# One attention layer and one retention layer in split fp32: residual loads, first-group loads, a v split, moves on ScalarE and squares in two parts

## The chip, the cores and the metric

The kernel runs on one core of one Trainium2 chip. A core has five engines that run their own instruction streams and meet at semaphores: TensorE (PE; its weight loads are listed apart as PEld), VectorE (DVE), ScalarE (ACT), GpSimd (POOL) and SyncE (SP). Of SP only the DMAs that it issues matter here; POOL issues DMAs too. The metric is device microseconds (us) of one execution, the median of 3 runs; lower is better.

## The reference

Batch 1, 512 tokens, width 2048, two layers. What is computed:

```python
# layer 0: gated grouped-query attention, 16 heads of 128, 4 k/v heads
proj = h @ w_in                                   # 2048 -> q 2048, k 512, v 512, g 2048
q = apply_rope(rms_norm(q, q_gain), cos, sin) * (A_HEAD_DIM ** -0.5)
k = apply_rope(rms_norm(k, k_gain), cos, sin)
s = q k^T ; p = softmax(s) ; o = p v              # in blocks of 128 queries
y = (o * jax.nn.silu(g)) @ w_out
x = layer_norm(ALPHA * x + y, ln_gain[0], ln_bias[0])
# layer 1: gated bidirectional retention, 8 heads, q/k 256, v 512
proj = h @ w_in                                   # 2048 -> q 2048, k 2048, v 4096, g 4096
o = forward scan(q, k, v) + backward scan(q, k, v)
y = (head_group_norm(o) * jax.nn.silu(g)) @ w_out
x = layer_norm(ALPHA * x + y, ln_gain[1], ln_bias[1])
```

All is fp32, and the layer norms keep mean and variance of a row of 2048 elements: `mean((x - mu)**2)` with `mu = mean(x)`.

## The kernel before

**Products.** Every fp32 operand is split into a high part `hi` (rounded to fp32r by a ScalarE cast, L114) and a low part `lo = x - hi` (a VectorE subtraction, L115), and a product is three matmuls, hi·hi, lo·hi and hi·lo (`mm3`, L232 to L234). Weights come in chunks of 128x1024 fp32 (512 KB): `raw_load` (L122) asks for a chunk on SP's queue, `onto` (L126) adds another quarter to it with a DMA that POOL issues, `make_chunk` splits it into `whi` and `wlo`, and 12 matmuls of 512 columns use it. `next_chunk` makes chunks up to AHEAD = 2 ahead of the one in use; `wp` holds three split chunks, `rp` nine raw ones. The large input products are done blockwise by a seven-product scheme: each block of 1024 output columns is worked off as products 1 to 7 in the order (1, 5, 6, 3, 7, 2, 4), each of 4 chunks, 7 x 4 x 12 matmuls in all; L160 and L162 add weight quarters on VectorE, L277 to L283 add input quarters, and `spill` adds the results up.

**Order of work.** The order on TensorE is the order in which the program is written. For the other engines a scheduler sets it when the kernel is built, from the same program and its own estimates; each engine then works strictly in that order, so an instruction that waits holds up all that stand behind it on its engine.

**Stages.** (1) Layer 0's input product, blocks `a_in`; q, k, v and g are stored to DRAM. (2) Attention: `Group.load_kv` and `load_q` read them back and split them (k, v and q tiles), while `work`, a stream of leftover products, is pumped between the attention's steps so that TensorE has work; `work.pump(us)` takes so many microseconds of it, counted as MM3 = 0.68 per triple of matmuls. The last block of `a_in` is the stream under group 0. (3) Layer norm 1 (`norm_1`): its result is stored to `nD`, turned by TensorE transposes, and moved from PSUM to SBUF with gain and bias in `turn_1`, 128x256 at a time: 16 moves for each half r of the tokens, of which the odd k go to VectorE (L823) and the even to ScalarE (L826). `x2.form` then adds quarters (L277 to L283). (4) Layer 1's input product, 12 blocks `r_in`: for each pair of heads two q/k/v blocks and one gate block. `residual_2` hangs on four of these blocks through `hook`: for a slice c of 512 columns and a token tile t it loads gain and bias of layer norm 1 (for t = 0, L836) and the stored `nD` (L839), multiplies and adds on VectorE (L837, L840, L841) and stores ALPHA times the normed x to `yD2` (L842, issued by POOL), onto which the output products add later. It hangs on blocks 2 to 5, before the third chunk of product 1, 6, 3 or 2. (5) The heads (`Head.run`): `s_unit` makes a strip of scores and splits it (pTh, pTl), `o_unit` multiplies with v; `v.split` splits the two v tiles (inh, inl). Heads 0 and 1 run with the last `r_in` block as their stream, the others with output products. (6) The last output product in four token tiles, each with layer norm 2 right behind it (`norm_2`): sums of the rows come with the additions (`add`, L386), the squares from ScalarE (L421), `1/sqrt` from a POOL power (L450); z = (y - mu) gain on VectorE (L1023), y = z rstd + bias (L1026), then the store.

**Lines that the change touches.** L846 `hook(r_in[2 + c], (1, 6, 3, 2)[t], 2, residual_2, c, t)`; L749 `work.pump(31.5 * MM3)` ahead of `groups[0].load_kv()`; L822 `if k % 2:` in `turn_1`; L983 `if kb > 1 and len(self.v.tiles) < 2:` in `Head.run`; L411 to L424 `mean_rstd`.

Of the kernel before, what the change touches and what calls it, by code (L numbers as in the profile page):

```python
# [50 lines left out]
def encoder_trunk_kernel(  # L51
# [313 lines left out]
    class Sum:  # L365


        def __init__(self, quick=()):

            self.y, self.st, self.rows, self.quick = {}, {}, [], quick  # L370

        def load(self, src, halves=(0, 1)):
            for i in halves:
# [7 lines left out]
        def add(self, t, c, ps, scale, last=False):  # L381
# [9 lines left out]
                nc.vector.tensor_add(y, ps, y)  # L391
            if last and t in self.quick:
                nc.vector.bn_stats(self.st[t][:, 6 * c:6 * c + 6], y)

        def out_proj(self, og, scale, cols=(0, 1, 2, 3), last=False):

            for c in cols:
# [11 lines left out]
                for t in range(NT):  # L409
                    self.add(t, c, banks[t], scale, last)  # L410

        def mean_rstd(self, t):

            if t in self.quick:
                return mean_rstd(self.st[t])
            mu, neg, sq, rstd = small("k_rs", 4)[:, 0:1], small("nmr"), small("sm", 4), small("rstd")
            nc.vector.tensor_reduce(out=mu, in_=self.st[t][:, :4], axis=AX.X, op=ALU.add)
            nc.vector.tensor_scalar_mul(neg, mu, -1.0 / D)
            nc.vector.tensor_scalar_mul(mu, mu, 1.0 / D)
            for c in range(4):  # L420
# [390 lines left out]
    def turn_1(r, m):  # L811
# [7 lines left out]
        for k in (2 * m, 2 * m + 1):  # L819
            o = 256 * (k % 2)  # L820
            f = x2.quarter(r, kh, i)[:, k % 4]
            if k % 2:  # L822
                nc.vector.tensor_scalar(f, b[:, o:o + 256], lnt[:, 0, k:k + 1], lnt[:, 1, k:k + 1],  # L823
                                        op0=ALU.mult, op1=ALU.add)
            else:
                nc.scalar.activation(f, b[:, o:o + 256], AF.Identity, scale=lnt[:, 0, k:k + 1], bias=lnt[:, 1, k:k + 1])  # L826
        if r == 0 and m % 2:
            x2.form(1 + kh, i)

    def residual_2(c, t, gb={}):  # L830

        cs = slice(c * 512, c * 512 + 512)
        if t == 0:
            for n in ("ln_gain", "ln_bias"):
                gb[n] = temp(n)
                nc.sync.dma_start(out=gb[n], in_=a[n][0, cs].partition_broadcast(P))  # L836
            nc.vector.tensor_scalar_mul(gb["ln_bias"], gb["ln_bias"], ALPHA)  # L837
        f = temp("res")
        nc.sync.dma_start(out=f, in_=nD[:, t, cs])  # L839
        nc.vector.scalar_tensor_tensor(out=f, in0=f, scalar=ALPHA, in1=gb["ln_gain"], op0=ALU.mult, op1=ALU.mult)  # L840
        nc.vector.tensor_add(f, f, gb["ln_bias"])  # L841
        nc.gpsimd.dma_start(out=yD2[:, t, cs], in_=f)  # L842
# [68 lines left out]
    class Head:  # L911
# [240 lines left out]
```

## Time and profile before

| | us |
|---|---|
| median of 3 runs | 2148.22 (2147.92 to 2150.19) |
| the profiled execution, its own time | 2150.57 |
| its span, first to last instruction | 2148.8 |
| PE busy in the span | 2108.5 (98%) |
| DVE busy | 1604.8 (75%) |
| ACT busy | 1100.8 (51%) |
| POOL busy | 377.2 (18%) |

TensorE is busy almost throughout, so the time is its work plus the places where it stands still or runs at a lower clock. A timeline row gives an instruction's start, its duration, and in brackets how long the engine sat idle before it and what ended that. Matmuls overlap, so their pace is read from start to start, not from durations. The profiled execution took 2.35 us more than the median.

### The profile page before, as it was taken

What the parts mean: (1) busy time and instruction counts of PE and PEld (TensorE: products, weight loads), DVE (VectorE), ACT (ScalarE), POOL (GpSimd) and SP (SyncE); (2) the same over time, 40 slices, a digit from 0 to 9 for tenths busy, and PEclk for the clock granted to TensorE, in tenths of its full rate; (3) what the DMA queues carried; (4) which work ended last, traced back from release to release, by engine and by line L of the source; (5) the groups of instructions that cost most, each with busy time, mean ns of one, the idle gap of its engine ahead of it and who ended that gap; (6) DMA issues with size and microseconds to landing.
All of it is one profiled execution on the core that took longest, in us unless ns stands there. A gap on an engine that the chain in (4) does not pass through costs nothing.

```text
span 2148.8 us, 26395 instructions
## 1 busy us (share of the span) xinstructions
PE 2108.5 (98%) x9744; PEld 1739.3 (81%) x9744; DVE 1604.8 (75%) x2185; ACT 1100.8 (51%) x1453; POOL 377.2 (18%) x449
## 2 busy tenths in 40 slices
PE   8999999999999999999999999999999999999997
PEld 7778887888888877788888888888888778888886
DVE  7787877877767896667877676766686787979766
ACT  5555545664543564444444444444455666656432
POOL 0333432010000122121112111111111122212200
PEclk9999999999999999999999999999999999999999
DMA  9976656563223578677676585585575668877862
GB/s 355 193 183 143 193 152 152 157 226 103 84 79 108 187 168 202 183 225 171 191 215 173 147 210 143 131 221 155 119 221 145 193 158 201 178 190 176 211 199 79
DMA packets 115634, 371.91 MB, mean 173 GB/s; under 512 B 14129, under 2 KB 17201, under 8 KB 115505
## 3 DMA queue, kind: packets, MB, share of 16 engines
q0 software_dynamic: 45568, 148.92, 33.6%
q1 hardware_dynamic: 69504, 220.39, 31.0%
q8 instruction: 76, 1.25, 0.2%
q10 hardware_dynamic: 432, 0.92, 0.1%
q14 instruction: 54, 0.43, 0.1%
HBM read 309.35 MB, written 60.82 MB: 172 GB/s over the span
## 4 chain that ended last, share of the span: by engine, by line
PE 74%; DMA 10%; issue 7%; DVE 6%; POOL 2%; ACT 2%; POOLq 0%; SPq 0%; ACTq 0%; DVEq 0%
PE acc L233 21%; PE acc L234 21%; PE acc L232 21%; DMA raw<-in_wa_in_dram 4%; DMA raw<-in_wr_in_dram 3%; PE tr L467 2%; DVE wlo L115 2%; PE o L233 2%; PE o L234 2%; PE o L232 2%; ACT whi L114 1%; PE s L234 1%; PE s L232 1%; PE s L233 1%; DMA q<-qD 1%
## 5 line engine op out<-in xcount | busy, mean ns | idle before, releaser
L115 DVE TENSOR_TENSOR wlo<-raw,whi 128x1024 fp32r<-128x1024 f32 (+1 forms) x598 | 726.4, 1217 | 331.7 <-ACT whi L114 327.1
L114 ACT CAST whi<-raw 128x1024 fp32r<-128x1024 f32 (+1 forms) x598 | 625.3, 1049 | 668.5 <-PE acc L234 537.1
L232 PE MATMUL acc<-whi,f 128*128 128x512 f32 x2240 | 882.9, 394 | 8.2 <-ACT whi L114 8.1
L233 PE MATMUL acc<-wlo,f 128*128 128x512 f32 x2240 | 877.1, 392 | 13.7 <-DVE wlo L115 13.3
L234 PE MATMUL acc<-whi,f 128*128 128x512 f32 x2240 | 875.2, 391 | 0.0
L233 PEld LDWEIGHTS acc<-wlo,f 128*128 128x128 f32 x2240 | 422.3, 189 | 108.5 <-DVE wlo L115 23.6
L232 PEld LDWEIGHTS acc<-whi,f 128*128 128x128 f32 x2240 | 422.1, 188 | 95.2 <-ACT whi L114 9.8
L234 PEld LDWEIGHTS acc<-whi,f 128*128 128x128 f32 x2240 | 421.7, 188 | 88.5
L126 POOL DMA_DIRECT2D raw<-in_wr_in_dram x104 | 90.1, 867 | 391.5 <-DVE wlo L115 238.9
L232 PE MATMUL acc<-whi,ogh 128*128 128x512 f32 x288 | 115.7, 402 | 0.5 <-ACT ogh L114 0.4
L234 PE MATMUL acc<-whi,ogl 128*128 128x512 f32 x288 | 112.7, 391 | 0.0
L233 PE MATMUL acc<-wlo,ogh 128*128 128x512 f32 x288 | 112.5, 391 | 0.0
L162 DVE TENSOR_TENSOR raw<-raw,raw 128x1024 f32<-128x1024 f32 x64 | 78.1, 1221 | 38.6 <-DMA raw<-in_wr_in_dram 34.3
L160 DVE TENSOR_TENSOR raw<-raw,raw 128x1024 f32<-128x1024 f32 x80 | 97.7, 1222 | 10.7 <-DMA raw<-in_wr_in_dram 7.6
L348 ACT COPY t<-acc 128x512 f32<-128x512 f32 x138 | 79.0, 588 | 48.4 <-PE acc L234 44.0
L450 POOL TENSOR_TENSOR rstd<-rs_e,neg_half 128x1 f32<-128x1 f32 x40 | 28.4, 711 | 368.4 <-DVE rs_e L449 367.3
L677 ACT ACTIVATE p<-s,nmax,q_rs 128x512 f32<-128x512 f32 x64 | 49.9, 780 | 36.6 <-DVE nmax L675 28.2
L450 POOL TENSOR_TENSOR q_rs<-rs_e,neg_half 128x4 f32<-128x4 f32 x16 | 45.1, 2820 | 113.0 <-DVE rs_e L449 113.0
L234 PEld LDWEIGHTS acc<-whi,ogl 128*128 128x128 f32 x288 | 54.0, 188 | 12.2 <-DVE ogl L115 0.4
L115 DVE TENSOR_TENSOR f<-xf,f 128x1024 fp32r<-128x1024 f32 (+2 forms) x52 | 59.9, 1156 | 5.4 <-ACT f L114 5.4
L232 PEld LDWEIGHTS acc<-whi,ogh 128*128 128x128 f32 x288 | 54.2, 188 | 10.8 <-ACT ogh L114 0.8
L126 POOL DMA_DIRECT2D raw<-in_wa_in_dram x48 | 44.2, 956 | 103.7 <-DVE wlo L115 70.0
(175 smaller groups left out, 2376.8 us busy)
## 6 DMA issues: line engine op xcount, KB each, us to landing
raw<-in_wr_in_dram SPq DMA_DIRECT2D x152, 512.0 KB, 4.7
raw<-in_wr_in_dram POOLq DMA_DIRECT2D x104, 512.0 KB, 6.0
raw<-in_wa_in_dram SPq DMA_DIRECT2D x66, 512.0 KB, 5.5
raw<-in_wa_in_dram POOLq DMA_DIRECT2D x48, 512.0 KB, 7.4
raw<-in_wr_p_dram SPq DMA_DIRECT2D x36, 512.0 KB, 5.2
raw<-in_wa_o_dram SPq DMA_DIRECT2D x32, 512.0 KB, 3.5
raw<-in_wr_p_dram POOLq DMA_DIRECT2D x24, 512.0 KB, 7.1
yD<-t POOLq DMA_DIRECT2D x36, 256.0 KB, 6.8
```

The source lines that it names most:

```text
L114: nc.scalar.copy(hi, src)
L115: nc.vector.tensor_sub(lo, src, hi.bitcast(F32))
L126: nc.gpsimd.dma_start(out=x, in_=src, accum_op=ALU.add)
L160: nc.vector.tensor_add(v, v, g[3, c])
L162: nc.vector.tensor_add(v, v, g[2, c])
L232: nc.tensor.matmul(ps, sh, mh, start=start, stop=False, skip_group_check=go_on)
L233: nc.tensor.matmul(ps, sh, ml, start=False, stop=False, skip_group_check=go_on)
L234: nc.tensor.matmul(ps, sl, mh, start=False, stop=stop, skip_group_check=go_on)
L348: nc.scalar.copy(keep[p, t], bk[CHAIN[p]][t])
L450: nc.gpsimd.tensor_tensor(out=dst, in0=e[:, :n], in1=neg_half[:, :n], op=ALU.pow)
L467: nc.tensor.transpose(out=b[:, tcols(i)], in_=src[:, tcols(i)], identity=ident)
L677: nc.scalar.activation(pt, sb, AF.Exp, scale=rs, bias=nmax, accum_out=self.sm[:, h:h + 1])
```

## The change

It does five things. The load half of `residual_2` becomes `load_residual`; slice c now hangs on block 3 + c, loads before the first chunk of products 1, 6, 3, 2 and arithmetic before the first chunk of 5, 3, 7, 4 (tiles 0 to 3). The pump ahead of group 0's loads is cut in two, 22.0 and 9.5: k, v and the first q tile are asked for after the first part. In `turn_1` VectorE keeps only every fourth move in the second half (r = 1); ScalarE does the others. Head 1 (and 0) may split v after score strip 1 rather than 2. For layer norm 2 the squares of columns 0 to 2 are taken about the mean of these three slices, as soon as they are there, the fourth slice's about the same mean, and the variance is set right by the square of the difference of the means.

```diff
+            elif last and c == 2:
+                self.squares_to(t)
...
+        def square(self, t, c):
+            neg, sq = self.about[t]
+            nc.scalar.activation(temp("sq"), self.y[t, c], AF.Square, bias=neg, accum_out=sq[:, c:c + 1])
...
+        def squares_to(self, t):
+
+            neg = small("nmax")
+            self.about[t] = neg, small("sm", 4)
+            nc.vector.tensor_reduce(out=neg, in_=self.st[t][:, :3], axis=AX.X, op=ALU.add)
+            nc.vector.tensor_scalar_mul(neg, neg, -1.0 / (3 * 512))
+            for c in range(3):
+                self.square(t, c)
...
-            nc.vector.tensor_scalar_mul(neg, mu, -1.0 / D)
             nc.vector.tensor_scalar_mul(mu, mu, 1.0 / D)
-            for c in range(4):
-                nc.scalar.activation(temp("sq"), self.y[t, c], AF.Square, bias=neg, accum_out=sq[:, c:c + 1])
+            nc.vector.tensor_add(d, mu, neg)
+            nc.vector.tensor_mul(d, d, d)
             nc.vector.tensor_reduce(out=neg, in_=sq, axis=AX.X, op=ALU.add)
-            rsqrt(rstd, neg, 1.0 / D, LN_EPS)
+            nc.vector.scalar_tensor_tensor(out=neg, in0=neg, scalar=1.0 / D, in1=d, op0=ALU.mult, op1=ALU.subtract)
+            rsqrt(rstd, neg, 1.0, LN_EPS)
...
-    work.pump(31.5 * MM3)
+    work.pump(22.0 * MM3)
     groups[0].load_kv()
     groups[0].load_q(0)
+    work.pump(9.5 * MM3)
     groups[0].load_q(1)
...
-            if k % 2:
+            if k % 2 and (r == 0 or k % 4 == 1):
...
+    def load_residual(c, t):
...
+        res[t] = temp("res")
+        nc.sync.dma_start(out=res[t], in_=nD[:, t, cs])
...
-            hook(r_in[2 + c], (1, 6, 3, 2)[t], 2, residual_2, c, t)
+            hook(r_in[3 + c], (1, 6, 3, 2)[t], 0, load_residual, c, t)
+            hook(r_in[3 + c], (5, 3, 7, 4)[t], 0, residual_2, c, t)
...
-                if kb > 1 and len(self.v.tiles) < 2:
+                if kb > (1 if self.h > 1 else 0) and len(self.v.tiles) < 2:
```

The order on TensorE stays the same, instruction for instruction. On the other engines it changes at these places.

VectorE ahead of group 0, before: `k`, `v` and `q` are the split tiles, `kv` and `q` also the loaded ones, `raw`, `whi`, `wlo` the weight chunks.

```order
L115 TENSOR_TENSOR wlo_2766<-raw_2596,whi_2765 128x1024
L160 TENSOR_TENSOR raw_2596<-raw_2596,raw_2784 128x1024
L115 TENSOR_TENSOR wlo_2788<-raw_2518,whi_2787 128x1024
L162 TENSOR_TENSOR raw_2518<-raw_2518,raw_3132 128x1024
L115 TENSOR_TENSOR wlo_2815<-raw_2546,whi_2814 128x1024
L115 TENSOR_TENSOR k_2832<-kv_2834,k_2832 128x512
L115 TENSOR_TENSOR v_2833<-kv_2838,v_2833 128x512
L115 TENSOR_TENSOR q_2843<-q_2842,q_2843 128x512
```

The same place after:

```order
L115 TENSOR_TENSOR wlo_2766<-raw_2596,whi_2765 128x1024
L115 TENSOR_TENSOR k_2781<-kv_2783,k_2781 128x512
L115 TENSOR_TENSOR v_2782<-kv_2787,v_2782 128x512
L115 TENSOR_TENSOR q_2792<-q_2791,q_2792 128x512
L115 TENSOR_TENSOR wlo_2805<-raw_2518,whi_2804 128x1024
L160 TENSOR_TENSOR raw_2596<-raw_2596,raw_2801 128x1024
L162 TENSOR_TENSOR raw_2518<-raw_2518,raw_3132 128x1024
L115 TENSOR_TENSOR wlo_2832<-raw_2546,whi_2831 128x1024
```

The three splits stand four instructions of 128x1024 further ahead. The order in which SP issues the loads of this place does not change.

VectorE in head 1, before: `f` are score strips, `inl` the low parts of the two v tiles.

```order
L941 SCALAR_TENSOR_TENSOR f_13591<-s_13584,strip_13278 128x512
L162 TENSOR_TENSOR raw_12871<-raw_12871,raw_13548 128x1024
L115 TENSOR_TENSOR pTl_13567<-f_13591,pTh_13566 128x512
L941 SCALAR_TENSOR_TENSOR f_13607<-s_13600,strip_13278 128x512
L115 TENSOR_TENSOR wlo_13614<-raw_13459,whi_13613 128x1024
L115 TENSOR_TENSOR pTl_13569<-f_13607,pTh_13568 128x512
L941 SCALAR_TENSOR_TENSOR f_13631<-s_13624,strip_13278 128x512
L115 TENSOR_TENSOR inl_13621<-raw_13538,inh_13620 128x1024
```

The same place after, from the same score strip on:

```order
L966 SCALAR_TENSOR_TENSOR f_13591<-s_13584,strip_13278 128x512
L115 TENSOR_TENSOR inl_13599<-raw_13538,inh_13598 128x1024
L966 SCALAR_TENSOR_TENSOR f_13611<-s_13604,strip_13278 128x512
L115 TENSOR_TENSOR pTl_13567<-f_13591,pTh_13566 128x512
L115 TENSOR_TENSOR wlo_13618<-raw_13459,whi_13617 128x1024
L115 TENSOR_TENSOR pTl_13569<-f_13611,pTh_13568 128x512
L966 SCALAR_TENSOR_TENSOR f_13635<-s_13628,strip_13278 128x512
L115 TENSOR_TENSOR inl_13625<-raw_13540,inh_13624 128x1024
L115 TENSOR_TENSOR pTl_13569<-f_13635,pTh_13568 128x512
```

The first v split stands six places further ahead, the second before the last strip's low part, and L162, which adds a weight quarter, behind all of them.

VectorE at the last token tile, before, from the sum of the row sums on (`k_rs`, the mean) to the first results:

```order
L417 TENSOR_REDUCE k_rs_17701<-ln_st_17657 128x1
L418 TENSOR_SCALAR nmr_17702<-k_rs_17701 128x1
L419 TENSOR_SCALAR k_rs_17701<-k_rs_17701 128x1
L1023 SCALAR_TENSOR_TENSOR z_17720<-y_16846,k_rs_17701,ln_gain_17382 128x512 x2
L1023 SCALAR_TENSOR_TENSOR z_17721<-y_17058,k_rs_17701,ln_gain_17384 128x512 x2
L422 TENSOR_REDUCE nmr_17702<-sm_17703 128x1
L449 TENSOR_SCALAR rs_e_17717<-nmr_17702 128x1
```

The same place after:

```order
L434 TENSOR_REDUCE k_rs_17728<-ln_st_17672 128x1
L435 TENSOR_SCALAR k_rs_17728<-k_rs_17728 128x1
L436 TENSOR_TENSOR nmr_17729<-k_rs_17728,nmax_17702 128x1
L1048 SCALAR_TENSOR_TENSOR z_17740<-y_16846,k_rs_17728,ln_gain_17382 128x512
L437 TENSOR_TENSOR nmr_17729<-nmr_17729 128x1
L438 TENSOR_REDUCE nmax_17702<-sm_17703 128x1
L1048 SCALAR_TENSOR_TENSOR z_17740<-y_16846,k_rs_17728,ln_gain_17382 128x512
L439 SCALAR_TENSOR_TENSOR nmax_17702<-nmax_17702,nmr_17729 128x1
L1048 SCALAR_TENSOR_TENSOR z_17741<-y_17058,k_rs_17728,ln_gain_17384 128x512
L466 TENSOR_SCALAR rs_e_17737<-nmax_17702 128x1
L1048 SCALAR_TENSOR_TENSOR z_17741<-y_17058,k_rs_17728,ln_gain_17384 128x512
```

The sum of the squares (L422, now L438) moves ahead of three of the four z, and two more small instructions stand among them.

## Rows read from the trace of the kernel before

**Rows 1.** The page: its first line, and PE's line of the part on busy time (us, share of the span, instructions).

```profile
span 2148.8 us, 26395 instructions
PE 2108.5 (98%) x9744; PEld 1739.3 (81%) x9744; DVE 1604.8 (75%) x2185; ACT 1100.8 (51%) x1453; POOL 377.2 (18%) x449
```

**Rows 2.** The list of waits, of PE alone: line of the waiting instruction, who ended the wait, us in total, times, longest.

```profile
PE acc L233 <- DVE wlo L115: 13.3, 16, 2.9
```

**Rows 3.** Busy time in stretches of 10 us: the stretch, its length, busy us (instructions) of PE, PEld, DVE, ACT and POOL, the granted TensorE clock (1.00 is 2.4 GHz), the DMA engines' busy share, GB/s.

```profile
350.00:360.00 10.00, 7.99 (x26) 5.72 (x25) 6.83 (x11) 5.93 (x10) 0.00 (x0) 0.83 0.20 52
...
780.00:790.00 10.00, 7.46 (x32) 5.39 (x33) 10.00 (x12) 5.77 (x7) 2.96 (x4) 1.00 0.73 131
...
860.00:870.00 10.00, 10.00 (x48) 8.29 (x47) 4.25 (x5) 4.70 (x5) 1.89 (x3) 1.00 1.02 279
870.00:880.00 10.00, 7.08 (x25) 5.37 (x24) 6.08 (x7) 2.08 (x3) 2.86 (x4) 0.83 0.72 208
...
1670.00:1680.00 10.00, 7.04 (x30) 5.04 (x29) 9.82 (x16) 9.29 (x15) 0.80 (x1) 1.00 0.70 225
```

**Rows 4.** Timeline at the start of group 0, SP, PE and DVE.

```profile
331.07 0.34 SPq L661 DMA_DIRECT2D q<-qD  x1
...
345.74 1.23 DVE L115 TENSOR_TENSOR wlo<-raw,whi 128x1024 fp32r<-128x1024 f32 x1 [0.95 <-ACT whi L114]
...
350.59 0.50 PE L232 MATMUL s<-k,q 128*128 128x512 f32 x1
...
351.67 0.68 DVE L115 TENSOR_TENSOR k<-kv,k 128x512 fp32r<-128x512 f32 x1
...
352.41 0.50 PE L233 MATMUL s<-k,q 128*128 128x512 f32 x1 [1.31 <-DVE k L115]
...
353.61 0.78 PE L234 MATMUL s<-k,q 128*128 128x512 f32 x1 [0.70 <-DVE q L115]
...
357.37 0.40 PE L234 MATMUL acc<-whi,f 128*128 128x512 f32 x1
```

**Rows 5.** Timeline in block 2 of `r_in`, where the first residual tile is worked.

```profile
863.11 0.46 SPq L839 DMA_DIRECT2D res<-nD  x1
...
869.34 0.43 DVE L837 TENSOR_SCALAR ln_bias<-ln_bias 128x512 f32<-128x512 f32 x1 [3.52 <-DMA ln_bias<-in_ln_bias_dram]
869.43 0.39 PE L232 MATMUL acc<-whi,f 128*128 128x512 f32 x1
...
871.47 0.39 PE L232 MATMUL acc<-whi,f 128*128 128x512 f32 x1
...
872.89 0.69 DVE L840 SCALAR_TENSOR_TENSOR res<-res,ln_gain 128x512 f32<-128x512 f32 x1 [3.13 <-DMA res<-nD]
873.50 1.22 DVE L115 TENSOR_TENSOR wlo<-raw,whi 128x1024 fp32r<-128x1024 f32 x1
...
874.78 0.50 PE L233 MATMUL acc<-wlo,f 128*128 128x512 f32 x1 [2.92 <-DVE wlo L115]
...
879.46 0.39 PE L234 MATMUL acc<-whi,f 128*128 128x512 f32 x1
```

**Rows 6.** The moves of `turn_1` (all of a line: count, ns min/median/max, first and last start), then the timeline of the dense stretch behind them.

```profile
L823 DVE TENSOR_SCALAR xf<-tr,lnt x16: 534/537/542, 713.1 to 755.9; 128x256 f32<-128x256 f32 x16
...
L826 ACT ACTIVATE xf<-tr,lnt x16: 544/560/571, 712.4 to 754.7; 128x256 f32<-128x256 f32 x16
...
741.47 1.23 DVE L115 TENSOR_TENSOR wlo<-raw,whi 128x1024 fp32r<-128x1024 f32 x1 [1.53 <-ACT whi L114]
...
779.37 0.39 PE L232 MATMUL acc<-whi,f 128*128 128x512 f32 x1
...
791.84 0.38 PE L467 MATMUL tr<-ident,m 128*128 128x128 f32 x2
```

**Rows 7.** Timeline in head 1, at its first `o_unit`.

```profile
1666.26 1.23 DVE L162 TENSOR_TENSOR raw<-raw,raw 128x1024 f32<-128x1024 f32 x1 [2.37 <-DMA raw<-in_wr_in_dram]
...
1670.35 0.50 PE L232 MATMUL o<-inh,pTh 128*128 128x512 f32 x1
...
1670.94 1.21 DVE L115 TENSOR_TENSOR inl<-raw,inh 128x1024 fp32r<-128x1024 f32 x1
...
1676.74 0.39 PE L232 MATMUL acc<-whi,f 128*128 128x512 f32 x1
```

**Rows 8.** Timeline of the last token tile, behind TensorE's last matmul.

```profile
2137.29 0.69 DVE L386 SCALAR_TENSOR_TENSOR y<-y,acc 128x512 f32<-128x512 f32 x1 [1.31 <-PE acc L234]
...
2138.40 0.72 ACT L421 ACTIVATE sq<-y,nmr 128x512 f32<-128x512 f32 x1 [7.88 <-DVE nmr L418]
2138.59 2.74 DVE L1023 SCALAR_TENSOR_TENSOR z<-y,k_rs,ln_gain 128x512 f32<-128x512 f32 x4
...
2141.36 0.16 DVE L422 TENSOR_REDUCE nmr<-sm 128x1 f32<-128x4 f32 x1
...
2142.43 2.74 DVE L1026 SCALAR_TENSOR_TENSOR y<-z,rstd,ln_bias 128x512 f32<-128x512 f32 x4 [0.72 <-POOL rstd L450]
```

**Rows 9.** Blocks 4 and 5 of `r_in`, which have a residual before and after: SP's residual and raw loads of block 4, and the one place in block 5 where TensorE waits.

```profile
1041.12 24.13 SPq L839 DMA_DIRECT2D res<-nD  x4
1087.87 31.25 SPq L122 DMA_DIRECT2D raw<-in_wr_in_dram  x12
...
1182.59 0.50 PE L233 MATMUL acc<-wlo,f 128*128 128x512 f32 x1 [1.33 <-DVE wlo L115]
```

More of the change, by code (lines that the diff above doesn't have):

```diff
@@ L368, in __init__ @@
         def __init__(self, quick=()):
-            self.y, self.st, self.rows, self.quick = {}, {}, [], quick
+            self.y, self.st, self.rows, self.quick, self.about = {}, {}, [], quick, {}
         def load(self, src, halves=(0, 1)):
@@ L415, in mean_rstd @@
                 return mean_rstd(self.st[t])
-            mu, neg, sq, rstd = small("k_rs", 4)[:, 0:1], small("nmr"), small("sm", 4), small("rstd")
+            self.square(t, 3)
+            (neg, sq), mu, d, rstd = self.about[t], small("k_rs", 4)[:, 0:1], small("nmr"), small("rstd")
             nc.vector.tensor_reduce(out=mu, in_=self.st[t][:, :4], axis=AX.X, op=ALU.add)
-            nc.vector.tensor_scalar_mul(neg, mu, -1.0 / D)
             nc.vector.tensor_scalar_mul(mu, mu, 1.0 / D)
-            for c in range(4):
-                nc.scalar.activation(temp("sq"), self.y[t, c], AF.Square, bias=neg, accum_out=sq[:, c:c + 1])
+            nc.vector.tensor_add(d, mu, neg)
+            nc.vector.tensor_mul(d, d, d)
             nc.vector.tensor_reduce(out=neg, in_=sq, axis=AX.X, op=ALU.add)
-            rsqrt(rstd, neg, 1.0 / D, LN_EPS)
+            nc.vector.scalar_tensor_tensor(out=neg, in0=neg, scalar=1.0 / D, in1=d, op0=ALU.mult, op1=ALU.subtract)
+            rsqrt(rstd, neg, 1.0, LN_EPS)
             return mu, rstd
@@ L828, in turn_1 @@
             x2.form(1 + kh, i)
-    def residual_2(c, t, gb={}):
+    res = {}
+    def load_residual(c, t):
         cs = slice(c * 512, c * 512 + 512)
@@ L834, in residual_2 @@
             for n in ("ln_gain", "ln_bias"):
[L835 to L842, printed above, removed]
+                res[n] = temp(n)
+                nc.sync.dma_start(out=res[n], in_=a[n][0, cs].partition_broadcast(P))
+        res[t] = temp("res")
+        nc.sync.dma_start(out=res[t], in_=nD[:, t, cs])
+    def residual_2(c, t):
+        f = res.pop(t)
+        if t == 0:
+            nc.vector.tensor_scalar_mul(res["ln_bias"], res["ln_bias"], ALPHA)
+        nc.vector.scalar_tensor_tensor(out=f, in0=f, scalar=ALPHA, in1=res["ln_gain"], op0=ALU.mult, op1=ALU.mult)
+        nc.vector.tensor_add(f, f, res["ln_bias"])
+        nc.gpsimd.dma_start(out=yD2[:, t, c * 512:c * 512 + 512], in_=f)
     for c in range(4):
         for t in range(NT):
-            hook(r_in[2 + c], (1, 6, 3, 2)[t], 2, residual_2, c, t)
+            hook(r_in[3 + c], (1, 6, 3, 2)[t], 0, load_residual, c, t)
+            hook(r_in[3 + c], (5, 3, 7, 4)[t], 0, residual_2, c, t)
     def rope_2(t, src, put):
```

## The prediction

> **What bounds the kernel now.** I read the page first: TensorE is busy 2108.5 of 2148.8 us [rows 1], so at most 40.3 us of standing still are to be had, and besides these only places where it runs at a lower clock. Next the list of PE's waits: the costliest group is that for VectorE's low parts of the weights, 13.3 us in 16 waits, the longest 2.9 [rows 2]. Then the span cut into stretches of 10 us, to find where these waits lie. Four stretches carry the bulk: PE is busy 7.99, 7.46, 7.08 and 7.04 of 10 us [rows 3]. In two of them the granted clock is 0.83 too, a mean of its two levels 2.4 and 1.2 GHz, after PE had stood idle; what such a wait costs is therefore more than the wait. So I price a place from matmul to matmul: at full clock they start (871.47 - 869.43) / 9 = 0.227 us apart over ten matmuls [rows 5], and what a stretch takes beyond its count times 0.227 is lost there. The start of the kernel also loses time, but the change does not touch it. Last I read the timeline around each place and the new order on the engines.
>
> **The change part by part.** The order on TensorE is the same, so every term is a wait that goes or comes.
>
> *Group 0.* From the first score matmul at 350.59 the twelfth matmul starts at 357.37; eleven steps should take 2.49 us, they took 6.78: 4.29 lost, of it 1.31 + 0.70 waiting for the low parts of k and q and the rest at the lower clock [rows 3, 4]. The data were not late: VectorE reached k's split at 351.67 only because four 128x1024 instructions stood ahead of it. In the new order k, v and q stand right behind the wlo of 345.74, which lasts 1.23 us [rows 4]: three splits of 0.68 end at 349.0 at the latest, before 350.59. The wlo of the next chunk behind them, 1.23 more, is there at 350.2 and first needed after the three score matmuls, near 351.3. So the wait goes, with it the slow stretch: **-4.29**. Bounds: nothing, if the casts on ScalarE find their data missing that early, to the whole.
>
> *Residual.* In block 2 VectorE sat idle 3.52 us for the bias and 3.13 us for the tile, whose load, issued at 863.11, was used at 872.89; the wlo behind these ran at 873.50 and PE waited 2.92 us for it [rows 5]. From 871.47 the fifteenth matmul starts at 879.46: 7.99 us for fourteen steps, which should take 3.17, so 4.82 lost. After the change nothing of the residual stands in block 2; the wlo can follow its cast, and PE has no reason to stop: **-4.82** (3.0 to 4.82, since the earlier PE may find the next chunk's load late). Blocks 3 to 5 have slices 1 to 3 before and 0 to 2 after, at almost the same points of VectorE's and SP's order, so I cost that at nothing. Block 6 gets a residual that it did not have: two adds of 0.69 us for each of four tiles, 1 MB in tiles, 0.5 MB gain and bias, 1 MB stored. VectorE has room there; the price is a weight load that comes later. The nearest row is block 5, where PE waits 1.33 us [rows 9]. Bounds 0 to 1.33, taken in the middle, **+0.7**.
>
> That loads compete is in the rows: the stretch before the wait has a DMA share of 1.02 [rows 3]. The Trainium skill (DMA: Bandwidth & Descriptors, "Issuing engines are not separate DMA queues") says that loads issued from different engines share the same 16 DMA engines and interleave; by that, a load asked for sooner only takes its place from a weight load, and the megabytes moved to block 6 should cost there what they cost in block 2. The sum by it would be 4.8 us worse; it is a rival below.
>
> *Moves.* Four VectorE moves of 0.537 us go to ScalarE at 0.560 [rows 6]. VectorE is busy 10.00 of 10 us where PE then waits, ScalarE 5.77 [rows 3]. From 779.37 to 791.84 there are 36 matmuls and one group of four transposes, counted as one and a half matmuls: 8.5 at full pace, 12.47 taken, 4.0 lost. VectorE has no idle time from 741.47 on, but had 1.53 just before [rows 6]; the first of the four moves lies before that, so three shorten the queue: 3 x 0.537 = **-1.6** (0 to 4 x 0.537 = 2.15). ScalarE's extra 2.24 us lie in its idle time; without that cover they would delay the casts and eat the gain. VectorE remains late by some 2.4 us.
>
> *v split.* From 1670.35 the thirteenth matmul starts at 1676.74: 6.39 against twelve steps, 2.72, so 3.67 lost. VectorE had waited 2.37 us for a weight load at L162 with v's low part behind it, which came at 1670.94 [rows 7]. In the new order the first v split follows the second strip; the pieces between, laid end to end from where VectorE's wait began (1666.26 - 2.37 = 1663.9), are one wlo and two splits of v of 1.2 and five strip pieces of 0.7: 7.1 us, so the last is done near 1671, when the matmul that needs it is the tenth from 1670.35, 1672.4. L162, now behind, finds its load landed, and PE has two chunks ready: **-3.67** (0 to 3.67).
>
> *Squares.* The last tile's sums are there at 2137.29 + 0.69; four squares on ScalarE (2138.40 on) end when the four z do, 2141.36, and y starts at 2142.43 [rows 8]. With three squares taken before, ScalarE is done some 1.9 us sooner. But in the new order VectorE has seven small instructions, of 0.16 us like L422's, and the four z, 2.74, between the row sums and y, with the power beside the last z: 2137.98 + 1.1 + 2.74 = 2141.8, and some 0.03 between any two small ones, so 2142.1. I take **-0.3**, by VectorE; bounds -1.9 (ScalarE alone) and +0.2. What is late next is VectorE.
>
> Sum: -4.29 - 4.82 + 0.7 - 1.6 - 3.67 - 0.3 = -14.0. The profiled execution took 2150.57, so 2136.6 for its like; it lies 2.35 above the median of the runs, 2148.22, so **2134.2 us** by the median.
>
> **The rivals.**
> *The residual's stall moves.* Block 6, or another, loses what block 2 lost, 4.82 in place of 0.7: 2138.3. For it: the DMA share at 1.02 and block 5's 1.33 [rows 3, 9]. Against: loads and arithmetic now lie four chunks, 48 matmuls or 10.9 us, apart, and a load took under 9.8 us where it was worst [rows 5].
> *Group 0's split waits all the same*, that is, the change does not do what it says: SP issues these loads in the old order, and if the tiles land after 346 us the splits, now ahead of the weight chunks, wait: 2138.5. For it: the order on SP. Against: SP issued k and v, and then q at 331.07, 14.7 us ahead of that wlo [rows 4].
> *DMA takes back the gains of moves and residual.* Between 779 and 880 PE runs up to 6.4 us earlier into stretches whose loads fill the engines [rows 3]: 2140.6. Against: at 780 to 790 and 870 to 880 the share is 0.73 and 0.72, so loads can start earlier too.
> *Slower: SP's queue is held by the residual loads.* A residual load that waits for a free temporary stands ahead of the weight loads. In block 4 these four issues spread over 24.13 us; the next raw load went out at 1087.87, 22.6 us after their end [rows 9]. Nothing is lost up to that point; every us of waiting beyond it is a us lost in each of four blocks. Loads asked for up to two chunks sooner and held longer take more temporaries; if they wait 28 us longer, 4 x 5.4 = 21.6 us are lost: 2155.8. Against: SP's order after shows the same grouping, four residual loads between twelves of raw loads.
>
> **How the numbers follow.** The forecast holds with 0.62; its own range is 2131.4 (all upper bounds: 4.29 + 4.82 + 2.15 + 3.67 + 1.9 = 16.8) to 2138. The moved residual stall 0.12, group 0 waiting 0.08, DMA taking back 0.08, two of these three together (2142.6 to 2144.9, counted as the same) 0.07, slower 0.03. A range from 2131 to 2142 leaves out the last two, 0.10, and what falls below. What a measurement of this kernel can tell from no change is about 0.2%, 4.3 us: faster means below 2143.9, 0.62 + 0.12 + 0.08 + 0.08 = 0.90; the same 0.07; slower 0.03.
>
> **What would show it.** Right: no matmul at half clock at 350 to 360 and 870 to 880, granted clock 1.00; PE's 2.92 us wait gone and no VectorE wait for a residual load; no wait for `inl`; in the dense stretch a loss of 2 to 3 us left, VectorE still full; behind the last matmul about 11.2 us to the end against 11.5. Wrong: a DMA as the end of a wait of k's split; PE waits over 2 us in blocks 3 to 6; SP's residual loads spread over more than 45 us; ScalarE's casts late at 750 to 760.

## The result and the profile after

The changed kernel takes 2135.73 us (median of 6 runs, 2134.75 to 2138.37); the kernel before took 2149.81 us beside it (median of 6, 2147.92 to 2154.01). The ratio is 0.9934, 95% interval 0.9921 to 0.9947, which is 14.2 us of 2149.81, between 11.4 and 17.0. The forecast was 2134.2 us, a gain of 14.0. The sum came out; by the experiments below, not all of its terms did.

The page of the changed kernel, its first line and PE's:

```profile
span 2133.0 us, 26407 instructions
PE 2103.3 (99%) x9744; PEld 1738.8 (82%) x9744; DVE 1602.0 (75%) x2197; ACT 1102.0 (52%) x1457; POOL 379.3 (18%) x449
```

PE stands still for 2133.0 - 2103.3 = 29.7 us, 10.6 less than in [rows 1]; the other 5.2 us of the shorter span are busy time that the same 9744 matmuls no longer take. The lower clock is a part of that: the stretches show it at two places before and at one after. The list of waits of PE has no k, q or `inl` left, and less for the weights than [rows 2]:

```profile
PE acc L233 <- DVE wlo L115: 9.7, 14, 1.8
```

Stretches of 10 us of the changed kernel, columns as in [rows 3]:

```profile
350.00:360.00 10.00, 10.00 (x48) 8.29 (x47) 6.58 (x10) 5.42 (x9) 0.00 (x0) 1.00 0.15 56
780.00:790.00 10.00, 8.69 (x40) 7.08 (x40) 9.17 (x9) 7.66 (x10) 4.16 (x5) 1.00 0.93 177
810.00:820.00 10.00, 8.16 (x29) 6.29 (x28) 6.40 (x7) 3.87 (x4) 1.14 (x2) 0.83 0.74 169
860.00:870.00 10.00, 10.00 (x46) 8.28 (x45) 5.42 (x6) 4.22 (x4) 2.51 (x4) 1.00 0.85 248
870.00:880.00 10.00, 10.00 (x46) 8.28 (x45) 4.36 (x4) 4.51 (x6) 2.11 (x3) 1.00 1.05 223
1240.00:1250.00 10.00, 9.20 (x39) 6.98 (x38) 8.81 (x9) 3.15 (x3) 0.00 (x0) 1.00 0.57 184
1655.00:1665.00 10.00, 10.00 (x46) 8.28 (x45) 10.00 (x16) 8.49 (x14) 0.00 (x0) 1.00 0.55 185
```

Group 0, block 2 and head 1 are full and at 2.4 GHz. 780 to 790 is better and not full; 810 to 820 has a lower clock that the kernel before did not have there; 1240 to 1250 is block 6, with a new loss. In the kernel before the same matmuls come some 7 and 12 us later:

```profile
810.00:820.00 10.00, 9.89 (x44) 7.87 (x42) 3.15 (x3) 3.14 (x3) 2.60 (x3) 1.00 1.01 280
820.00:830.00 10.00, 8.37 (x37) 6.94 (x38) 7.50 (x8) 4.80 (x6) 1.13 (x2) 1.00 0.63 167
1250.00:1260.00 10.00, 10.00 (x45) 8.26 (x45) 8.60 (x9) 4.22 (x4) 0.00 (x0) 1.00 0.65 206
```

Group 0's start in the changed kernel, PE and VectorE; it answers to [rows 4]:

```profile
346.77 0.68 DVE L115 TENSOR_TENSOR k<-kv,k 128x512 fp32r<-128x512 f32 x1
...
347.98 0.68 DVE L115 TENSOR_TENSOR q<-q,q 128x512 fp32r<-128x512 f32 x1
...
349.98 0.39 PE L232 MATMUL s<-k,q 128*128 128x512 f32 x1
350.20 0.39 PE L233 MATMUL s<-k,q 128*128 128x512 f32 x1
...
364.08 0.66 PE L484 MATMUL tr<-ident,p 128*128 128x128 f32 x4 [0.75 <-DVE pTl L115]
```

The splits stand where the forecast put them (done at 348.66), and the score matmuls follow each other without a wait. A new, shorter wait comes 14 us later, for a low part of the probabilities.

Block 6, VectorE, where the residual is new, and head 1 with its two v splits, which come before the matmuls that need them (compare [rows 9] and [rows 7]):

```profile
1239.84 1.23 DVE L162 TENSOR_TENSOR raw<-raw,raw 128x1024 f32<-128x1024 f32 x1 [3.14 <-DMA raw<-in_wr_in_dram]
...
1653.10 1.22 DVE L115 TENSOR_TENSOR inl<-raw,inh 128x1024 fp32r<-128x1024 f32 x1
...
1657.92 1.22 DVE L115 TENSOR_TENSOR inl<-raw,inh 128x1024 fp32r<-128x1024 f32 x1
```

In block 6 a weight load is late; the residual's loads themselves are not waited for. The tail, which answers to [rows 8]:

```profile
2121.57 0.39 PE L234 MATMUL acc<-wkh,ogl 128*128 128x512 f32 x1
...
2122.86 0.71 ACT L416 ACTIVATE sq<-y,nmax 128x512 f32<-128x512 f32 x1
...
2125.37 0.15 DVE L466 TENSOR_SCALAR rs_e<-nmax 128x1 f32<-128x1 f32 x1
2125.43 0.74 DVE L1048 SCALAR_TENSOR_TENSOR z<-y,k_rs,ln_gain 128x512 f32<-128x512 f32 x1
2126.61 2.74 DVE L1051 SCALAR_TENSOR_TENSOR y<-z,rstd,ln_bias 128x512 f32<-128x512 f32 x4 [0.43 <-POOL rstd L467]
```

ScalarE's last square starts at 2122.86 and could release the power near 2124; the power's input is formed on VectorE at 2125.37 only, behind three z; the power itself (0.43 us of VectorE's waiting) comes after it. As forecast, VectorE's order sets y.

### The profile page after: what moved, and what is told of

It is laid out like the page before. It is cut to its first block, busy times and chain, and to the rows that moved or that the text cites. A ratio compares the mean times of both kernels' runs of the same rounds, so it can differ in the third digit from the quotient of the medians.

```text
span 2133.0 us, 26407 instructions
## 1 busy us (share of the span) xinstructions
PE 2103.3 (99%) x9744; PEld 1738.8 (82%) x9744; DVE 1602.0 (75%) x2197; ACT 1102.0 (52%) x1457; POOL 379.3 (18%) x449
## 4 chain that ended last, share of the span: by engine, by line
PE 84%; DMA 7%; DVE 4%; issue 3%; ACT 1%; POOL 1%; POOLq 0%; SPq 0%; DVEq 0%; ACTq 0%
PE acc L233 24%; PE acc L234 24%; PE acc L232 24%; DMA raw<-in_wr_in_dram 3%; PE tr L484 3%; DMA raw<-in_wa_in_dram 3%; DVE wlo L115 2%; PE o L232 2%; PE o L234 2%; PE o L233 2%; PE s L234 1%; PE s L232 1%; PE s L233 1%; ACT whi L114 1%; POOL raw L126 1%
## 5 line engine op out<-in xcount | busy, mean ns | idle before, releaser
L162 DVE TENSOR_TENSOR raw<-raw,raw 128x1024 f32<-128x1024 f32 x64 | 78.1, 1221 | 38.0 <-DMA raw<-in_wr_in_dram 32.7
L160 DVE TENSOR_TENSOR raw<-raw,raw 128x1024 f32<-128x1024 f32 x80 | 97.5, 1221 | 10.6 <-DMA raw<-in_wr_in_dram 7.4
```

What stands on the lines that cost most here:

```text
L160: nc.vector.tensor_add(v, v, g[3, c])
L162: nc.vector.tensor_add(v, v, g[2, c])
```

## The experiments

All these kernels issue the same matmuls in the same order, so the k-th matmul of one profile can be set against the k-th of another. The table gives, for each profile, how much longer or shorter a stretch took than in the first profile of the kernel before, from matmul start to matmul start; a stretch is named by the times it has there (340 to 370 is group 0's start, 860 to 890 the stall in block 2, 1195 to 1280 block 6, 1640 to 1685 head 1). The first three blocks are worked with their products interleaved, up to 968; so 890 to 960 is still block 2, and 960 to 1195 is blocks 3 to 5. The tail is the time from the last matmul's start to the end.

```
                 340   370   770   800   860   890   960  1195  1640
               to370 to470 to800 to835 to890 to960  1195  1280  1685   tail    span
before          0.00  0.00  0.00  0.00  0.00  0.00  0.00  0.00  0.00  11.93  2148.8
e9 (before)    -2.15 -1.61  1.56 -1.38 -0.42  0.16  1.43  0.02 -0.21  11.94  2146.6
e1 group 0     -4.11 -2.30  1.41 -0.52 -1.55  0.07  2.44  0.02 -0.91  11.93  2143.1
e2 residual    -2.38 -1.61 -0.02 -0.61 -4.84 -0.81 -0.46  1.41  0.72  11.92  2144.1
e3 moves       -2.26 -0.77  0.19  2.60  0.03  0.07  0.94  0.32 -0.16  11.92  2148.0
e4 v split     -2.26 -2.48  0.00 -0.34  0.78  0.07  0.82  0.39 -4.18  11.94  2143.8
changed        -3.50 -2.32 -1.41  1.69 -4.84 -0.71 -0.49  1.39 -3.84  11.40  2133.0
e5 late ask    -4.39 -2.07  0.15  0.73 -4.84 -0.94  0.38  1.86 -3.18  11.42  2135.2
e6 block 2     -3.49 -2.56  0.11  0.23  0.21  0.03  1.62  0.27 -3.59  11.41  2140.1
e10 early      -4.46 -0.82 -1.41  0.64 -4.84  0.08  1.72  0.09 -3.99  11.41  2136.8
e7 all 8       -4.48 -2.71 -2.64 -0.28 -4.84 -0.61 -0.34  0.55 -4.38  11.40  2129.1
e11 no moves   -3.28 -1.07  1.45  0.53 -4.84 -0.59 -0.35  1.18 -4.34  11.41  2139.2
e8 squares     -4.42 -1.71  0.20  2.32 -4.82  0.16  0.84  0.98 -3.52  11.93  2140.5
e12 all 8+tail -3.74 -0.86 -2.70  3.69 -4.83 -0.52 -0.31  1.02 -3.36  12.35  2138.8
```

Some columns repeat to 0.05 us (the tail, and block 2 where the residual has left it); others scatter by 1 to 3 us between profiles of one piece of code (770 to 835). A term can be read from a column only with that scatter beside it. The columns do not add up to the spans: up to 340, where no edit reaches, the profiles lie between -0.6 and +4.1, and between 1685 and the last matmul between -1.5 and +1.7.

**The kernel before once more (e9).** No edit.

> The kernel before, unchanged, profiled once more. In the profiles of the residual, the moves and the v split alone, group 0 is as in the kernel before, but lost some 2.0 us at its first score matmuls in place of 4.29, with the granted clock at 1.00 in place of 0.83. Theory A (the lower clock there belonged to one execution): the new profile loses 2.0 to 2.5 us there, and the group 0 term of the prediction was twice too large. Rival B (the kernel before always has it, and something in those three edits took it away): 4 us or more, clock 0.83 again. In the stretch from 770 to 835 both expect what the profiles without the moves edit showed, within 1 us of the first profile.

It took 2153.03 us in the median of 12 runs, ratio to the kernel before 1.0011, interval 1.0001 to 1.0022: one and the same kernel, apart by 0.11%, and by more than the interval. Differences of that size between two kernels mean nothing here. Its profile at group 0 and at the dense stretch, PE's rows and the stretches:

```profile
352.13 0.50 PE L233 MATMUL s<-k,q 128*128 128x512 f32 x1 [0.81 <-DVE k L115]
353.34 0.50 PE L234 MATMUL s<-k,q 128*128 128x512 f32 x1 [0.70 <-DVE q L115]
...
785.71 0.50 PE L233 MATMUL acc<-wlo,f 128*128 128x512 f32 x1 [1.31 <-DVE wlo L115]
786.04 0.43 PE L234 MATMUL acc<-whi,f 128*128 128x512 f32 x1
786.27 0.63 PE L232 MATMUL acc<-whi,f 128*128 128x512 f32 x1
```

```profile
350.00:360.00 10.00, 8.49 (x35) 6.30 (x34) 6.63 (x11) 6.44 (x11) 0.00 (x0) 1.00 0.18 52
780.00:790.00 10.00, 7.58 (x24) 5.53 (x25) 10.00 (x12) 4.36 (x5) 3.98 (x5) 0.83 0.82 147
```

The two waits of [rows 4] are there, the first shorter by 0.5 us, and the clock stays at 1.00: 2.15 us less lost. Theory A holds; the lower clock in group 0 belonged to one execution. In the dense stretch it is the other way round: here the clock falls to 0.83, 1.56 us lost, behind a wait that in the first profile left the clock alone.

**Group 0 alone (e1).**

```diff
-    work.pump(31.5 * MM3)
+    work.pump(22.0 * MM3)
     groups[0].load_kv()
     groups[0].load_q(0)
+    work.pump(9.5 * MM3)
     groups[0].load_q(1)
```

> The kernel before with the group 0 edit alone. Theory A (each part pays at its own place, by itself): no wait for k or q at the first score matmuls, full clock there, 4.3 us won between the matmuls that started at 350.59 and 357.37; and since the softmax of group 0 runs ahead, the two short waits for p behind it (at 386 and 456 of the kernel before) go too, so about 5.8 us are kept at the matmul that started at 466, and about 5 to 6 us at the end: a time 0.9973 of before. Rival B (the win is passed on to the next wait): TensorE comes earlier into the stretches at 780, 820 and 870 whose loads fill the DMA engines, waits longer there by 2 us or more in all, and 3 us or less are kept at the end.

2147.66 us, ratio 0.9978 (0.9969 to 0.9988). Against the first profile 6.4 us are won up to 470, of which a lower clock at 780 to 790 takes 1.41 back: theory A, by that comparison. But the kernels that have group 0 in its old order (e9, e2, e3, e4) are also 2.2 to 2.4 better at 340 to 370. Over the five profiles with the old order the mean is -1.81, over the nine with the new one -3.99: the edit is worth 2.2 us there, with a doubtful 0.5 behind it.

**The residual alone (e2).** The diff's `load_residual`, `residual_2` and their hooks.

> The kernel before with the residual edit alone. Theory A: the wait of 2.92 us in block 2 goes with its slow stretch, 4.8 us won between the matmuls that started at 871 and 880; some 1.5 more in blocks 3 and 5, as in the changed kernel, and 1.4 lost in block 6, where the residual is new: 4.9 us kept. Rival B: the gain in block 2 in the changed kernel needed its earlier arrival (7 us of group 0 and moves); alone, the next chunk's load is late there and 3 us or less are won.

2145.61 us, ratio 0.9978 (0.9965 to 0.9990). Block 2 gives 4.84 without any help from the other parts, block 6 takes 1.41: theory A.

**Asked for late (e5).** The changed kernel; the loads stand at their arithmetic, one block later than before.

```diff
-            hook(r_in[3 + c], (1, 6, 3, 2)[t], 0, load_residual, c, t)
-            hook(r_in[3 + c], (5, 3, 7, 4)[t], 0, residual_2, c, t)
+            hook(r_in[3 + c], (1, 6, 3, 2)[t], 2, load_residual, c, t)
+            hook(r_in[3 + c], (1, 6, 3, 2)[t], 2, residual_2, c, t)
```

> The changed kernel, its residual one block later as it is, but each load asked for where its arithmetic is, at chunk 2 of products 1, 6, 3 and 2. Theory A (the sooner asking matters): VectorE waits for the bias and for each first tile as it did in block 2 of the kernel before (3.5 and 3.1 us), now in block 3, and PE loses some 3 to 5 us there: 3 to 5 us slower than the changed kernel. Rival B (leaving block 2 is what paid, since its stretch was short of DMA time): no PE wait above 1 us in blocks 3 to 6, and within 1.5 us of the changed kernel.

2137.04 us, ratio 0.9937 (0.9922 to 0.9952), as the changed kernel's. No VectorE instruction of the residual waits for its load; PE's waits in blocks 5 and 6 are 1.37 and 1.20 us, slightly above the 1 us that rival B allowed. SyncE's issue of the first load, in the changed kernel and then in this one:

```profile
951.62 0.44 SPq L855 DMA_DIRECT2D ln_gain<-in_ln_gain_dram  x1
```

```profile
952.58 0.38 SPq L855 DMA_DIRECT2D ln_gain<-in_ln_gain_dram  x1
```

PE is 0.9 us later there too (its matmul of 935.09 starts at 936.01): the load was not asked for later at all. SyncE issues its 472 DMAs in one and the same order in both kernels, and VectorE's order differs only from 1035 us on; the scheduler undid the edit. So theory A was not put to the test. What the run does show is that the sooner asking of the changed kernel, which stands in the program, is not in the executed order: there the gain came from leaving block 2.

**In block 2, asked for ahead (e6).** The changed kernel with `r_in[2 + c]` in both hooks.

> The changed kernel, its loads asked for four chunks ahead as it does, but in blocks 2 to 5 as before, so that block 6 has no residual. Theory A (asking sooner is enough): no VectorE wait for a residual load in block 2, the 4.8 us stay won, and the 1.4 us that block 6 cost come back: 1.4 us faster than the changed kernel. Rival B (a load asked for sooner only takes its place from a weight load in a stretch whose DMA engines are full): PE waits 2 us or more for a weight chunk in block 2, 3 to 5 us slower than the changed kernel at the matmul that started at 880 before, of which 1.4 come back in block 6.

2141.92 us, ratio 0.9959 (0.9946 to 0.9973): the gain of block 2 is gone (+0.21). Rival B had the place and the size right and the cause wrong: VectorE waits for the residual's own loads. Nor is this a test of asking ahead: SyncE's order is again, DMA for DMA, that of the kernel before, and the tile's load goes out at the same matmul as there. VectorE, PE and SyncE in block 2:

```profile
857.01 0.42 SPq L857 DMA_DIRECT2D res<-nD  x1
...
863.79 0.43 DVE L863 TENSOR_SCALAR ln_bias<-ln_bias 128x512 f32<-128x512 f32 x1 [4.22 <-DMA ln_bias<-in_ln_bias_dram]
866.84 0.69 DVE L864 SCALAR_TENSOR_TENSOR res<-res,ln_gain 128x512 f32<-128x512 f32 x1 [2.63 <-DMA res<-nD]
...
868.72 0.51 PE L233 MATMUL acc<-wlo,f 128*128 128x512 f32 x1 [3.12 <-DVE wlo L115]
```

**In block 2, asked for in block 1 (e10).** As e6, with the first three loads eight chunks sooner.

```diff
+            if c == 0 and t == 0:
+                hook(r_in[1], 3, 0, load_residual, c, t)
```

> The residual in blocks 2 to 5, as in the run of that name before, but its first loads (gain, bias, tile 0) asked for eight chunks sooner, in block 1. Theory A (SP comes to them too late, behind weight loads that wait for their buffers): asked for 20 us ahead, they have landed, VectorE waits for neither, PE's wait of 3.1 us goes, and the stretch from 860 to 890 takes 4.8 us less than with the residual in block 2. Rival B (the DMA engines are full there, whatever comes first): the weight chunks come later instead and PE still loses 2 us or more between 835 and 890.

This time SyncE's order does change: it issues the tile's load 26.6 us sooner than in e6. The load lands at 835.18, in a stretch with a DMA share of 0.85 (829 to 836), and VectorE finds it there; the share is 1.03 to 1.06 only later (840 to 860):

```profile
830.45 0.38 SPq L857 DMA_DIRECT2D res<-nD  x1
...
848.13 0.42 DVE L863 TENSOR_SCALAR ln_bias<-ln_bias 128x512 f32<-128x512 f32 x1
...
850.37 0.68 DVE L864 SCALAR_TENSOR_TENSOR res<-res,ln_gain 128x512 f32<-128x512 f32 x1
```

2138.39 us, ratio 0.9941 (0.9925 to 0.9957). Block 2 is at -4.84 again, and block 6 costs nothing (0.09): theory A. Block 2 can carry the residual if its first loads go out early enough, here ahead of the stretch in which the DMA engines are full; a load issued within that stretch and in time was not tried. VectorE's arithmetic on the first tile stands 72 matmuls further ahead too, but the tile had landed 13 us before it. The full 4.8 us come back by either way. By the Trainium skill (DMA: Bandwidth & Descriptors, "Issuing engines are not separate DMA queues") the early loads should, as the prediction read it, have taken their time from weight loads; no such cost is seen here. (The prediction's 4.8 us for it leaves out that 0.7 was in the sum already; its rival has the right 4.1.)

**The moves: alone (e3), all eight (e7), none (e11).** e3 has the edit alone, e11 is the changed kernel without it, e7 has

```diff
-            if k % 2 and (r == 0 or k % 4 == 1):
+            if k % 2 and r == 0:
```

> The kernel before with four moves on ScalarE alone. Theory A: 1.4 us won between the matmuls that started at 779 and 792, as in the changed kernel, and kept: the 1.3 us that the changed kernel lost behind its wait at 814 is an accident of the clock and has nothing to do with the moves, so no lower clock behind the wait that ended at 821.63. Rival B: the stretch around 815 waits for a load that comes when it comes; arriving earlier lengthens that wait, the clock falls behind it, and by the matmul that started at 833 nothing of the 1.4 us is left.

> The changed kernel with the other four moves of the second half on ScalarE too. Theory A (VectorE's queue sets the dense stretch, 0.54 us each): 1.5 to 2.1 us less lost at 779 to 792. Rival B (ScalarE's casts are late by now, or the win stops at the next late load): less than 0.5 us won at the matmul that started at 833 before, or a loss.

> The changed kernel with the four moves back on VectorE. Theory A (the moves won their 1.4 to 1.6 us, as the profile of the changed kernel shows): without them 1.4 us or more lost between the matmuls of the kernel before at 770 and 800, and the time 0.07% above that of the changed kernel. Rival B (the shorter wait that is left lets the clock fall, which takes it all back, as in four of the five profiles with the moves edit): the stretch from 770 to 835 takes no longer than in those five, where it took 1.4 us more than in the kernel before on average.

Times: e3 2149.14 us, ratio 0.9989 (0.9978 to 1.0000); e7 2137.13, 0.9931 (0.9916 to 0.9945); e11 2137.52, 0.9946 (0.9931 to 0.9961). None can be told from its neighbour by time. By place, from 770 to 800: six profiles without the edit have 0.73 on average (0 or 1.4 to 1.6), six with four moves -0.36 (-1.41 or 0.1 to 0.2), two with eight -2.67. Within a set the lower values have a granted clock of 1.00 from 780 to 790, the higher ones 0.83 to 0.85. From 800 to 835 it turns round: -0.39 without, 1.37 with four. Over both stretches 0.35 (-0.63 to 1.98) stands against 1.01 (-0.77 to 2.79). So VectorE's queue is shortened as forecast, and on average the win does not last 35 us. At a like clock the four moves are worth 1.3 to 1.4 us at 770 to 800. PE's wait near 821 of the kernel before then grows from 1.3 us on average (0.34 to 2.24) to 2.2 (1.83 to 2.45), and the clock falls there in three of the six profiles with the edit and in none without. Stretches of e3, and the load that VectorE waits for in the second of them:

```profile
780.00:790.00 10.00, 8.16 (x30) 6.03 (x29) 9.11 (x10) 5.63 (x6) 3.27 (x4) 0.83 0.83 151
810.00:820.00 10.00, 7.55 (x31) 5.69 (x30) 3.66 (x5) 2.09 (x2) 0.97 (x2) 0.96 0.94 199
820.00:830.00 10.00, 10.00 (x40) 8.12 (x39) 5.67 (x6) 4.89 (x6) 1.00 (x2) 0.87 0.39 117
```

```profile
816.54 1.23 DVE L160 TENSOR_TENSOR raw<-raw,raw 128x1024 f32<-128x1024 f32 x1 [6.34 <-DMA raw<-in_wr_in_dram]
```

The first has fewer and shorter waits than [rows 3], and the lower clock; the second waits for a load under a DMA share of 0.94, and the third pays for that with a lower clock. e3 fits rival B. e7 fits its theory A by place, with 1.23 us won on the changed kernel in place of 1.5 to 2.1, and keeps them to 835; but its profile is the fastest of its six runs, and e12, with the same moves, loses them. e11 fits neither cleanly: 1.45 us are lost at 770 to 800, as theory A had it, and its 1.98 over both stretches lies above the mean of the five profiles that rival B named, 1.36, and inside their range.

**The v split alone (e4).**

```diff
-                if kb > 1 and len(self.v.tiles) < 2:
+                if kb > (1 if self.h > 1 else 0) and len(self.v.tiles) < 2:
```

> The kernel before with the earlier v split alone. Theory A: both waits for the low part of v in head 1 go, 3.7 us won between the matmuls that started at 1670 and 1677, and all of it is kept. Rival B: the split stood behind a weight chunk whose load was late, and in the changed kernel that load was only early because everything before it ran 12 us sooner; alone, VectorE waits for the load all the same, PE waits for the chunk, and 2 us or less are won.

2146.57 us, ratio 0.9977 (0.9965 to 0.9990); PE has no wait left in head 1, -4.18. Theory A.

**The squares undone (e8).** The changed kernel with `mean_rstd` of the kernel before.

> The changed kernel with the four squares taken together again, as before. Theory A: only the tail changes; y starts 5.6 us behind the last matmul where the changed kernel has 5.0, so 0.5 us slower. Rival B: the three early squares also delayed something ahead of the tail, and nothing or less than 0.2 us is lost without them.

The tail is 11.93 in place of 11.40, as theory A had it. The time, 2141.86 us, ratio 0.9958 (0.9945 to 0.9970), is some 5 us above the changed kernel's, in all five runs (2141.39 to 2142.34). But of the 7.5 us by which its profile is longer, 2.8 lie before 340, 1.6 at 770 to 800 and 2.2 at 890 to 1195, places that the edit doesn't touch: on every engine the order of the instructions ahead of the first undone square is the same. As a measure of the squares the time is useless; the tail is not. It also says how far to trust a difference in time between two builds: 5 us, as much as e1, e2 or e4 gains, can come without an instruction out of place, and what makes them was not found. Those three are therefore read by place.

**All eight moves and a lighter tail (e12).** e7, and in the last tile's last slice

```diff
+            if t == NT - 1 and c == 3:
+                nc.scalar.activation(z[c], z[c], AF.Identity, scale=rstd)
+                nc.gpsimd.tensor_add(y, z[c], lnp[1][c])
```

> The changed kernel with all eight moves of the second half on ScalarE, and the last slice of the last token tile finished by ScalarE and GpSimd beside VectorE. Theory A (with eight moves VectorE's queue lets no wait above 0.9 us at 770 to 800, so the clock stays at full speed there): that stretch 2.6 us shorter than before, and 10.8 us from the last matmul's start to the end in place of 11.4: faster than the changed kernel by 2 to 4 us, 0.991 of before. Rival B (its first profile was a lucky one): a wait of 1.3 us and the lower clock come back at 780, or the wait near 815 grows by as much, and the time is that of the changed kernel.

2136.24 us, ratio 0.9941 (0.9925 to 0.9957): not faster than the changed kernel. The dense stretch gives 2.70 again, and 3.69 go at the next late load; the tail got longer, 12.35. This profile alone has a granted clock of 0.95 for its first half, in full stretches too (790 to 800), at no visible cost in pace (0.5 us from 470 to 770). PE near 815, then VectorE and GpSimd in the tail:

```profile
816.84 0.66 PE L233 MATMUL acc<-wlo,f 128*128 128x512 f32 x1 [3.60 <-DVE wlo L115]
```

```profile
2131.54 3.08 DVE L1055 SCALAR_TENSOR_TENSOR y<-z,rstd,ln_bias 128x512 f32<-128x512 f32 x3 [0.44 <-POOL rstd L467]
```

```profile
2132.34 1.74 POOL L1053 TENSOR_TENSOR y<-z,ln_bias 128x512 f32<-128x512 f32 x1 [0.83 <-ACT z L1052]
```

Rival B. No version here beats the changed kernel by more than the measurement can tell.

## Why the prediction was right, and where it was not

Forecast -14.0, measured -14.2 (11.4 to 17.0). Means over all profiles with a part against those without it:

- *Group 0*, forecast -4.29. The mechanism is right, the size is not: -2.2 (profiles with the edit -3.28 to -4.48, without 0 to -2.38). The mis-sized step is pricing the place from matmul to matmul in one execution, the slow stretch included: that stretch is absent in the four other profiles of the old order, and their first wait is 0.5 to 0.7 us shorter. Some profiles also have the wait for `pTl` 14 us later, 0.75 us in the changed kernel, which the sum did not have.
- *Residual*, block 2, forecast -4.82: -4.82 to -4.84 in all seven profiles that have it out of block 2, -4.6 against the five others. "Nothing of the residual stands in block 2" was the reason, and it held: none of the seven has PE's wait of 2.9 us. But the four chunks between load and arithmetic, on which the rival was turned down, are not in the executed order: in block 3 the first tile's load goes out 40 matmuls ahead of its arithmetic, 41 in the kernel before. Block 6, forecast +0.7, bounds 0 to 1.33: 1.05, and up to 1.86 in one profile. The rest of block 2 (890 to 960), which the sum left out, gave 0.65; e6 and e10, whose other tiles still stand there, do not have it (0.03 and 0.08). Blocks 3 to 5, "at nothing": some 1.2 were won. Near 1018 PE waits 0.3 to 1.2 us in six of the seven profiles with the residual in blocks 2 to 5 and in none with it in 3 to 6; why was not tried.
- *Moves*, forecast -1.6: the changed kernel's profile shows -1.41 at the place, and over all profiles the place gives -1.1 (-1.3 to -1.4 at a like clock), but 800 to 835 gives it back (1.8 worse with the edit). Kept: nothing that can be measured, 0.66 lost by the means, within their scatter. The rival "DMA takes back" named this; the forecast gave it 0.08 and joined it to the residual, which kept all of its gain. The failed step is costing a win as kept where the next wait down the road is for a load. That the longer wait there comes from the earlier arrival is an inference from these means; e7, which keeps its win, speaks against a rule.
- *v split*, forecast -3.67: -3.7. Order and time of the pieces came as worked out.
- *Squares*, forecast -0.3: -0.52, the same within 0.03 in every profile, with VectorE's order as the limit; y starts 5.04 us behind the last matmul's start, 5.57 before.

With the moves at nothing these terms add to -2.2 - 4.6 - 0.65 - 1.2 + 1.05 - 3.7 - 0.5 = -11.8, near the lower end of the interval; with the doubtful 0.5 behind group 0, -12.3. The rest is within its width, and the base is no firmer: the one kernel before has medians of 2148.22 (3 runs), 2149.81 (6) and 2151.09 (35). That -14.0 hit the middle is partly luck: group 0 and the moves, 3.7 us too much together, stood in for the 1.9 us at 890 to 1195 and for what is left open. Of the rivals, group 0's split does not wait for data (done at 348.66), SP's queue is not held (the four residual loads of block 4 spread over 24.0 us in the changed kernel, 24.1 before), and no block took over the whole 4.82: PE's longest wait in its blocks 3 to 6 is 0.76 us.

## What to carry to other kernels

A stall priced from one execution contains that execution's clock: profile the unchanged kernel a second time before taking a stretch at half speed into the sum, and put kernels side by side instruction by instruction where the instruction order allows it. The wait for a load that moved away with its work was a gain in every profile here; a shortened queue ahead of a stretch that waits for DMA gave nothing that could be measured at the end. Writing a load earlier in the program does not ask for it earlier if the scheduler leaves it at its place in the queue, as in e5 and e6; look at the issue rows, not at the code.

## What was not expected of the hardware

The same wait may or may not bring the lower clock. In the first profile of the kernel before, PE waited 0.95 and 1.32 us and went on at 2.4 GHz:

```profile
789.18 0.50 PE L233 MATMUL acc<-wlo,f 128*128 128x512 f32 x1 [1.32 <-DVE wlo L115]
...
789.75 0.40 PE L232 MATMUL acc<-whi,f 128*128 128x512 f32 x1
```

In its second profile, after 0.95 and 1.31 us, the matmuls took 0.63 (rows at e9 above), and 1.56 us went. Near 815 a wait of 1.83 us brought it in the changed kernel (granted clock 0.83 from 810 to 820), and at the same matmul one of 2.39 us in e10 did not (1.00 from 810 to 830). The changed kernel, then e10:

```profile
814.02 0.50 PE L233 MATMUL acc<-wlo,f 128*128 128x512 f32 x1 [1.83 <-DVE wlo L115]
```

```profile
815.40 0.50 PE L233 MATMUL acc<-wlo,f 128*128 128x512 f32 x1 [2.39 <-DVE wlo L115]
```

The Trainium skill (TensorE: Matmul & The Clock Gate, "The HAM clock gate") says of a kernel's start that the stretch in which the chip looks at PE's activity runs freely, so that one kernel differs from run to run. These rows show such a difference in the middle of a kernel; that it has this cause, they do not show.

VectorE slows down beside GpSimd: three instructions of L1055 take 3.08 us while GpSimd adds (2132.34 to 2134.08, rows at e12), where four take 2.74 without it. The time is lost in the third alone:

```profile
2132.87 1.75 DVE L1055 SCALAR_TENSOR_TENSOR y<-z,rstd,ln_bias 128x512 f32<-128x512 f32 x1
```

The first two take 0.75 and 0.74 us. ScalarE's part was over at 2132.26, before the third began, so it is not the cause. The Trainium skill (Advanced Engine Details and Errata, "VectorE Performance Modes") says that VectorE's second port is shared with GpSimd; the rows agree, but they do not show the port, and this is one place in one run.
